# First group's output projection by Strassen pairs of 288 columns, with up weights formed beside the query pairs

## The chip, the cores and the metric

One core of a Trainium2 chip runs the kernel in one launch. The metric is the device time in microseconds (us), as the median of three runs. Of the core's engines the text names PE (TensorE, which multiplies matrices), DVE (VectorE), ACT (ScalarE), POOL (GpSimd) and SP (SyncE, whose queue issues nearly all DMAs here). Each engine works through its own instructions in order and waits on the others by semaphores.

## The reference

One decoder layer in float32 for a prompt of 1,024 tokens and a sample group of 8 x 8 tokens, which share the weights; the width is 1,024.

```python
h = rmsnorm(x, norm_mix)
q, k, v, gu, gv, ga, gb = split_in(h @ w_in)
o = attn_prompt(q, k, v, sinks)            # or attn_sample, for the sample group
vn = layernorm(jax.nn.gelu(gv), ln_g, ln_b)
s = spatial_gating(jax.nn.gelu(gu), vn, ws, bs)
merged = jax.nn.sigmoid(ga) * (o @ w_pa) + jax.nn.sigmoid(gb) * (s @ w_pb)
x = x + merged @ w_out
f, nconv = conv_ffn(rmsnorm(x, norm_ffn), w_up, conv_w, conv_b, w_down, prev)
return x + f, nk, nv, nconv, vn
```

The change is about `x + merged @ w_out`, the output projection.

## The kernel before

All activations are kept transposed: a tile has 128 of the 1,024 channels on its partitions and tokens along its columns. The 1,088 tokens are two groups: group 0 has 576 columns (64 of the sample group, 512 of the prompt), group 1 has the other 512. A float32 operand is split into a high part, rounded by ACT (`split`, L40), and a low part, the rest, by DVE (L41). A product is three matmuls: high with high, low with high, high with low.

The stages follow one another on PE: values and gMLP values, then queries, keys, gMLP inputs and gates (L297), attention with the branch products between its pieces, the merges, the first group's output projection, the second group's, the up stage (L297), the down stage (L1734) and the final norm. L237 is the matmul line of `mm3`, which the merges and both output projections share.

The stages on L297 take the weights in pairs of 128 x 1,024 tiles and multiply by Strassen's scheme (Winograd's form). A pair has 7 products in place of 8; each product is 4 blocks (`kk`) of 3 matmuls over half of a group's columns: 288 for group 0, 256 for group 1. For that a pair's weights are added to four sums (`ws`, L176) and split to seven halves of 128 x 512, and the activations to four sums (`combine`, L259 to L262) and split to seven operands per `kk`. `Chain.product` collects the products in PSUM banks, with the names "adadaca": a bank that goes on accumulating must have been copied out by ACT (`keep`, L278) first.

`Weights` (`W`) keeps the weights in order: four raw tiles (`wraw`) are loaded ahead, and `W.get` forms the next splits (`wh`, `wl`) ahead of their use in four slots.

The merge of tile c of group 1 is 48 matmuls of 256 columns; DVE then multiplies by the gate (L1094) and adds the other branch (L1096), and `operand(1)` splits the result. At the same time a merged tile of group 0 comes back from DRAM in its two parts (`m` and `b`), is added (L1397) and is split whole by `operand(0)`. So the first group's projection finds eight pairs `mh`, `ml` of 576 columns. It goes over eight output tiles, 24 matmuls of 320 and 24 of 256 columns for each, and `x1_tile` adds the tile of x, stores it and adds its square to the norm's sum (L1413, L1423).

Beside the merges and the first projection, in `pair_load` and `pair_unit`, the weights of the first NPRE = 2 pairs of the up stage are added and split (`hl`), and stored in DRAM (`upd`), from where the up stage takes them as they are.

The order on each engine isn't written out: a scheduler in the framework places the instructions from the code's order, so that matmuls of several products can be mixed.

Of the kernel before, what the change touches and what calls it, by code (L numbers as in the profile page):

```python
# [6 lines left out]
F32 = mybir.dt.float32  # L7
F32R = mybir.dt.float32r
# [7 lines left out]
P = 128  # L16
D = 1024
KD = 8
# [16 lines left out]
def layer(tc, a):  # L35
# [11 lines left out]
    with ExitStack() as top:  # L47
# [219 lines left out]
        class Chain:  # L267
# [19 lines left out]
            def product(self, j, w):  # L287
# [11 lines left out]
                kept = self.kept  # L299
# [55 lines left out]
        with ExitStack() as ph1:  # L355
# [523 lines left out]

            mo, sso = [ExitStack(), ExitStack()], ExitStack()  # L880
# [89 lines left out]
            late["qk"] = poola("qk", 1, qko)  # L970

            def behind(at, j):

                if done:
                    done.pop(0)()
# [9 lines left out]
            for at, (pair, gs, whole) in enumerate(seq):  # L985
                if at == 6:
                    qko.close()
# [38 lines left out]
            pst = ph1.enter_context(tc.tile_pool(name="pst", bufs=1, space=PSUM, reuse_waits="tile"))  # L1026
            pmm = ph1.enter_context(tc.tile_pool(name="pmm", bufs=2, space=PSUM, reuse_waits="tile"))
            psm = ph1.enter_context(tc.tile_pool(name="psm", bufs=1, space=PSUM, reuse_waits="tile"))
# [50 lines left out]
            def merge(g, c, to, early=False):  # L1079
# [3 lines left out]
                def part(e, k0):  # L1083
                    def go():
                        if e == k0 == 0:
# [4 lines left out]
                            st["w"], st["ps"] = W.get(), acc2()  # L1090
# [249 lines left out]
            hmo = [ExitStack(), ExitStack()]  # L1340
            hmp = [hmo[g].enter_context(tc.tile_pool(name=f"hm{g}", bufs=1, reuse_waits="tile")) for g in (1, 0)][::-1]

            def operand(g):
                def go(c, t):
                    hl = tuple(hmp[g].tile([P, groups[g]["n"]], F32R, name=f"m{x}{c}") for x in "hl")
                    split(*hl, t)
                    ms[g].append(hl)
                return go

            pwo, pair = ExitStack(), {}  # L1350
            pwp = pwo.enter_context(tc.tile_pool(name="pw", bufs=1, reuse_waits="tile"))

            def pair_load(f):
                def go():
                    store()
                    for e, name in enumerate("ab"):
                        pair[name] = pwp.tile([P, KD, P], F32, name=f"r{name}")
                        nc.sync.dma_start(pair[name], wt(UP0 + f + NFF * e))
                return go

            def pair_unit(f, j):

                def go():
                    store()
                    ta, tb = pair["a"], pair["b"]
                    a11, a12, a21, a22 = ta[:, 0:4], ta[:, 4:8], tb[:, 0:4], tb[:, 4:8]
                    src = {0: a11, 5: a12, 6: a22}.get(j)
                    if src is None:
                        x, y = ((a21, a22), (pair.get("s1"), a11), (pair.get("s2"), a12), (a11, a21))[j - 1]
                        src = pair[f"s{j}"] = pwp.tile([P, 4, P], F32, name="s", bufs=2)  # L1370
                        V.tensor_add(src, x, y)
                    t = pwp.tile([P, 2, 4, P], F32R, name="hl", bufs=2)
                    split(t[:, 0], t[:, 1], src)
                    pair["store"] = upd[f][j], t.bitcast(F32)
                return go

            def store():
                if "store" in pair:
                    nc.sync.dma_start(*pair.pop("store"))

            held = {}

            def hold(c):
                if c < KD:
                    held[c] = [pwp.tile([P, 576], F32, name=x, bufs=3) for x in "mb"]
                    for x, src in zip(held[c], (msd[c], mbd[0][c])):
                        nc.sync.dma_start(x, src)
# [586 lines left out]
```

## Time and profile before

| what | us |
|---|---|
| median of three runs | 1519.96 |
| lowest, highest | 1518.12, 1522.0 |
| span of the profiled execution | 1514.1 |
| its own time, beside the span | not measured apart; the span is 5.9 below the median |
| PE busy in the span | 1494.2 |
| merges of group 1 from the second on | about 680 to 714 |
| first group's output projection | 714.2 to 765.0 |
| second group's output projection | 765.0 to 811.5 |
| up stage | 811.5 to 1271 |

The span is the time from the first to the last instruction of one execution; the measured time also holds what lies around it. A row of the timeline gives an instruction's start, its duration, its engine, its line, its kind, what it writes and reads by the names of the program, its shape, and in brackets how long the engine was idle before it and what ended that. Instructions of one engine overlap in their durations, so that their cost in a chain is the distance from one start to the next.

### The profile page before, as it was taken

The numbers are of one execution on the slowest core, as the hardware profiler recorded it, in microseconds if no ns is written. First come the engines' busy times: TensorE is split into PE (matmuls) and PEld (weight loads), VectorE is DVE, ScalarE is ACT, GpSimd is POOL, SyncE is SP. The second block draws the span as 40 slices with busy tenths as digits, with TensorE's granted clock in tenths as the row PEclk, the third lists the DMA queues.
The fourth block names the chain that finished last, engine by engine and source line by source line (L and its number), as shares of the span: only waits on it lengthen the run. The fifth ranks groups of instructions, "written<-read, shape, count | busy, mean of one in ns | idle before, by whom it ended". The sixth has DMA issues, their size and how long they took to land.

```text
span 1514.1 us, 31415 instructions
## 1 busy us (share of the span) xinstructions
PE 1494.2 (99%) x12194; PEld 1481.5 (98%) x12194; DVE 1160.7 (77%) x1917; ACT 821.6 (54%) x1745; POOL 269.5 (18%) x427
## 2 busy tenths in 40 slices
PE   9999999999999999999999999999999999999997
PEld 9999999999998999999999999999999999999997
DVE  6896778756545895989668888898899888785685
ACT  7565764454543774864444555555555556353562
POOL 0000012200020222330132221332232122000003
PEclk9999999999999999999999999999999999999999
DMA  8452557747659857749988323332233226973453
GB/s 291 158 186 110 178 181 254 232 134 271 232 182 312 270 164 230 233 169 306 330 282 283 129 107 124 110 126 108 94 138 109 91 74 229 368 244 97 124 180 133
DMA packets 137508, 286.70 MB, mean 189 GB/s; under 512 B 15248, under 2 KB 44368, under 8 KB 137360
## 3 DMA queue, kind: packets, MB, share of 16 engines
q1 hardware_dynamic: 133040, 280.62, 55.1%
q10 hardware_dynamic: 4320, 4.08, 0.8%
q8 instruction: 96, 1.57, 0.4%
q14 instruction: 52, 0.43, 0.1%
HBM read 195.76 MB, written 90.85 MB: 189 GB/s over the span
## 4 chain that ended last, share of the span: by engine, by line
PE 85%; DVE 4%; ACT 4%; issue 3%; DMA 3%; POOL 1%; SPq 0%; POOLq 0%; ACTq 0%; DVEq 0%
PE st L297 49%; PE mm L237 14%; PE dn L1734 10%; PE st L528 6%; PE sc L1227 1%; DMA wraw<-wt 1%; DVE wl L41 1%; ACT s L1250 1%; PE pt L1260 1%; POOL x L1799 1%; PE mx L836 1%; PE po L1288 1%; DMA sg1d<-z 1%; ACT wh L40 1%; DVE nm L1243 0%
## 5 line engine op out<-in xcount | busy, mean ns | idle before, releaser
L297 PE MATMUL st<-th,wh 128*128 128x256 f32 (+1 forms) x2128 | 610.3, 287 | 2.1 <-ACT k L278 1.5
L297 PE MATMUL st<-tl,wh 128*128 128x256 f32 (+1 forms) x2128 | 608.4, 286 | 0.0
L297 PE MATMUL st<-th,wl 128*128 128x256 f32 (+1 forms) x2128 | 608.0, 286 | 0.0
L297 PEld LDWEIGHTS st<-th,wh 128*128 128x128 f32 x2128 | 399.9, 188 | 3.6 <-ACT k L278 2.5
L297 PEld LDWEIGHTS st<-th,wl 128*128 128x128 f32 x2128 | 400.2, 188 | 0.0
L297 PEld LDWEIGHTS st<-tl,wh 128*128 128x128 f32 x2128 | 399.7, 188 | 0.0
L41 DVE TENSOR_TENSOR wl<-wraw,wh 128x512 fp32r<-128x512 f32 (+2 forms) x204 | 158.2, 789 | 35.2 <-ACT wh L40 32.0
L40 ACT CAST wh<-wraw 128x512 fp32r<-128x512 f32 (+2 forms) x204 | 139.5, 694 | 82.3 <-PE st L297 33.5
L1734 PE MATMUL dn<-th,wh 128*128 128x288 f32 (+1 forms) x616 | 176.7, 287 | 0.0
L1734 PE MATMUL dn<-tl,wh 128*128 128x288 f32 (+1 forms) x616 | 176.2, 286 | 0.0
L1734 PE MATMUL dn<-th,wl 128*128 128x288 f32 (+1 forms) x616 | 175.1, 284 | 0.0
L40 ACT CAST wh<-ws 128x512 fp32r<-128x512 f32 x160 | 98.3, 622 | 105.2 <-PE st L297 67.9
L41 DVE TENSOR_TENSOR wl<-ws,wh 128x512 fp32r<-128x512 f32 x160 | 110.6, 704 | 48.0 <-ACT wh L40 46.1
L1734 PEld LDWEIGHTS dn<-th,wl 128*128 128x128 f32 x616 | 115.9, 188 | 0.0
L1734 PEld LDWEIGHTS dn<-tl,wh 128*128 128x128 f32 x616 | 115.7, 188 | 0.0
L1734 PEld LDWEIGHTS dn<-th,wh 128*128 128x128 f32 x616 | 115.6, 188 | 0.0
L285 POOL TENSOR_TENSOR z<-kn,k 128x256 f32<-128x256 f32 (+1 forms) x32 | 30.1, 943 | 305.0 <-ACT kn L280 287.7
L40 ACT CAST th<-traw 128x544 fp32r<-128x544 f32 (+1 forms) x85 | 53.9, 642 | 48.7 <-PE dn L1734 34.4
L41 DVE TENSOR_TENSOR tl<-traw,th 128x544 fp32r<-128x544 f32 (+1 forms) x85 | 61.5, 730 | 20.8 <-ACT th L40 20.7
L237 PE MATMUL mm<-s,wh 128*128 128x256 f32 (+1 forms) x384 | 76.4, 294 | 0.0
L528 PE MATMUL st<-w2h,th 128*128 128x256 f32 x308 | 74.1, 282 | 0.2 <-ACT w2h L40 0.2
L237 PE MATMUL mm<-ol,wh 128*128 128x256 f32 (+1 forms) x256 | 73.5, 288 | 0.4 <-DVE ol L41 0.4
(294 smaller groups left out, 3159.3 us busy)
## 6 DMA issues: line engine op xcount, KB each, us to landing
wraw<-wt SPq DMA_DIRECT2D x133, 512.0 KB
traw<-td SPq DMA_DIRECT2D x77, 272.0 KB
td<-za SPq DMA_DIRECT2D x22, 544.0 KB
wraw<-wt SPq DMA_DIRECT2D x35, 256.0 KB
upd<-hl SPq DMA_DIRECT2D x14, 512.0 KB
td<-t SPq DMA_DIRECT2D x11, 544.0 KB
qd<-q SPq DMA_DIRECT2D x8, 576.0 KB
q<-qd SPq DMA_DIRECT2D x8, 576.0 KB
```

Of the source, the lines that this page charges most:

```text
L40: S.copy(hi, src)
L41: V.tensor_sub(lo, src, hi.bitcast(F32))
L237: PE.matmul(ps[:, lo:lo + c1 - c0], u[:, k, :], v[:, c0:c1], start=(clear and k == 0 and i == 0), stop=(k == nk - 1 and i == 2), skip_grou ...
L285: op(to, pick(x, to, lo, hi), pick(y, to, lo, hi))
L297: PE.matmul(ps, u[:, kk, :], v, start=first and kk + i == 0, stop=kk == 3 and i == 2, skip_group_check=True)
L528: PE.matmul(ps, u, v[:, k, :], start=k + i == 0, stop=k == KD - 1 and i == 2)
L836: PE.matmul(ps[:, P * i:P * i + P], vn[:, i], late["wst"][:, c, :], start=True, stop=True)
L1227: PE.matmul(ps[:, h, o0:256], q, kst[kv][:, e, k0:cur + P], start=e == 0, stop=e == 1)
L1250: S.activation(s[:, h], s[:, h], AF.Exp, bias=nm[:, h:h + 1], accum_out=dn[:, h:h + 1])
L1260: PE.transpose(pt[:, h * P:h * P + P], s[:, h, 0:P], ident)
L1288: PE.matmul(half(po, e), v[:, b - 1 + e], half(x, e), start=e == 0 and x is ph, stop=False, skip_group_check=True)
L1734: PE.matmul(place(m, e), u[:, m, :], v[:, lo:hi], start=new and i + k == 0 and (e == 0 or m % 2 == 0), stop=i == NU - 1 and k == 2, skip_g ...
```

## The change

The first group's projection is done by the Strassen scheme too. Class `Out` is a `Chain` with its own way of collecting: ACT copies four of the banks (`keep`), POOL adds these copies into the two tiles of x of the pair, and DVE adds the other three straight from PSUM. There are 4 pairs (output tiles p and p + 4) of 7 products of 12 matmuls of 288 columns. W holds four pairs and then eight whole tiles in place of sixteen whole tiles.

The operands `tmh`, `tml` (seven of 288 columns for each `kk`) are formed in the merges of group 1: `entire` adds the two parts of a tile as before, `form_sums` makes the four sums of two tiles, `form_split` splits 288 and 576 columns at once and 1,152 a little later. The tiles come in the order 0, 4, 1, 5, 2, 6, 3, 7, so that each second merge has what one `kk` needs. The last merge asks W for four splits ahead, the first pair's halves.

The sums and splits of the first two up pairs' weights move to the query pairs (`up_units`, positions 1 to 4 of that stage, one unit beside every second product), with smaller loads (`px`, `py`).

Three places show the new order. First DVE at the end of the merges and the start of the first projection, before (L1094 and L1096 are the merge's multiply and add; L1371 and `hl` belong to the up weights):

```order
L1094 TENSOR_TENSOR stg<-stg,mm 128x512
L41 TENSOR_TENSOR wl<-wraw,wh 128x1024
L1096 TENSOR_TENSOR stg<-stg 128x512
L1371 TENSOR_TENSOR s<-s,ra 128x512
L41 TENSOR_TENSOR wl<-wraw,wh 128x1024
L41 TENSOR_TENSOR ml_9808<-stg,mh_9807 128x512
L41 TENSOR_TENSOR hl<-s,hl 128x512
L1371 TENSOR_TENSOR s<-ra,rb 128x512
L1094 TENSOR_TENSOR stg<-stg,mm 128x512
L41 TENSOR_TENSOR wl<-wraw,wh 128x1024
L1096 TENSOR_TENSOR stg<-stg 128x512
```

And the same place now (L1142 and L1144 are the multiply and the add of the last merge, `t` the sums of `form_sums`, `tml` the low operands of `kk` 3):

```order
L259 TENSOR_TENSOR t_9946<-m 128x288
L260 TENSOR_TENSOR t_9946<-m 128x288
L41 TENSOR_TENSOR tml_9964<-m,tmh_9963 128x288
L41 TENSOR_TENSOR wl<-ws,wh 128x512
L261 SCALAR_TENSOR_TENSOR t_9946<-t_9946,m 128x288
L41 TENSOR_TENSOR tml_9964<-m,tmh_9963 128x576
L262 SCALAR_TENSOR_TENSOR t_9946<-t_9946,m 128x288
L1142 TENSOR_TENSOR stg<-stg,mm 128x512
L176 TENSOR_TENSOR ws<-wraw 128x512
L1144 TENSOR_TENSOR stg<-stg 128x512
L41 TENSOR_TENSOR tml_9964<-t_9946,tmh_9963 128x1152
L41 TENSOR_TENSOR ml_9998<-stg,mh_9997 128x512
```

The last of the first projection's operands now stands behind the last merge's multiply and add, where before the group's operands were done ahead of them.

On PE, the first matmuls of the projection, before:

```order
L237 MATMUL mm_9898<-mh0_9320,wh_9817 128x320
L237 MATMUL mm_9898<-ml0_9321,wh_9817 128x320
L237 MATMUL mm_9898<-mh0_9320,wl_9818 128x320
L237 MATMUL mm_9898<-mh1_9382,wh_9817 128x320
L237 MATMUL mm_9898<-ml1_9383,wh_9817 128x320
```

And now, from the 19th of its matmuls on (the bank `st_10010` belongs to the pair's first product, `st_10032` to its second, `st_10109` to its sixth):

```order
L297 MATMUL st_10032<-tmh2_9804,wl_9915 128x288
L297 MATMUL st_10109<-tmh0_9496,wh_10026 128x288
L297 MATMUL st_10109<-tml0_9497,wh_10026 128x288
L297 MATMUL st_10010<-tml3_9964,wh_9914 128x288
L297 MATMUL st_10010<-tmh3_9963,wl_9915 128x288
L297 MATMUL st_10032<-tmh3_9963,wh_9914 128x288
L297 MATMUL st_10032<-tml3_9964,wh_9914 128x288
L297 MATMUL st_10032<-tmh3_9963,wl_9915 128x288
```

The matmuls that need `kk` 3 (`tmh3`, `tml3`) are put behind some that don't.

On SP, at the start of the query pairs, before:

```order
L147 DMA wraw<-wt 128x1024 x4
L860 DMA qd_114<-q 256x1x512
L860 DMA qd_115<-q 256x1x512
L147 DMA wraw<-wt 128x1024 x2
L860 DMA qd_106<-q 128x1152
```

And now:

```order
L895 DMA px<-wt 128x512
L895 DMA py<-wt 128x512
L899 DMA upd_1_183<-phl 128x1024
L895 DMA py<-wt 128x512
L899 DMA upd_6_188<-phl 128x1024
L867 DMA qd_114<-q 256x1x512
L867 DMA qd_115<-q 256x1x512
L899 DMA upd_2_184<-phl 128x1024
L869 DMA qsd<-z_1736 128x64
L147 DMA wraw<-wt 128x1024 x2
```

The loads and stores of the up weights stand between the loads of the weights that are needed next.

The diff, cut to its core:

```diff
-            for at in (PA0, PA0, WO0, WO0):
+            for at in (PA0, PA0):
                 for c in range(8):
                     W.add(wt(at + c), KD)
+            for c in range(4):
+                W.add_pair(wt(WO0 + c), wt(WO0 + c + 4))
+            for c in range(8):
+                W.add(wt(WO0 + c), KD)
...
+            def up_units(pool):
+
+                q, hold = {}, []
+
+                def load(name, f, x):
+                    src = wt(UP0 + f + NFF * (x[1] == "2"))
+                    k = 4 * (x[2] == "2")
+                    q[name] = pool.tile([P, 4, P], F32, name=name)
+                    nc.sync.dma_start(q[name], src[:, k:k + 4])
+
+                def store():
+                    if hold:
+                        nc.sync.dma_start(*hold.pop())
+
+                def step(f, j, src, add, then):
+                    def go():
+                        store()
+                        if add:
+                            V.tensor_add(q["px"], q["px"], q["py"])
+                        t = pool.tile([P, 2, 4, P], F32R, name="phl")
+                        split(t[:, 0], t[:, 1], q[src])
+                        hold.append((upd[f][j], t.bitcast(F32)))
+                        for x in then:
+                            load(*x)
+                    return go
+
+                out = [lambda: [load("px", 0, "a21"), load("py", 0, "a22")]]
+                for f in range(NPRE):
+                    more = [("px", f + 1, "a21"), ("py", f + 1, "a22")] if f + 1 < NPRE else []
+                    out += [step(f, 1, "px", True, ()), step(f, 6, "py", False, [("py", f, "a11")]),
+                            step(f, 2, "px", True, ()), step(f, 0, "py", False, [("py", f, "a12")]),
+                            step(f, 3, "px", True, [("px", f, "a21")]), step(f, 5, "py", False, [("py", f, "a11")]),
+                            step(f, 4, "px", True, more)]
+                return out + [store]
+
...
+                if ahead and at > 0 and j % 2 == 0:
+                    ahead.pop(0)()
...
-                            st["w"], st["ps"] = W.get(), acc2()
+                            st["w"], st["ps"] = W.get(4 if g and c > 6 else 1, 2 if g and c > 5 else 3), acc2()
...
+            tw, held, raw = {}, {}, {}
+            half_of = lambda t: t.rearrange("p (h c) -> p h c", h=2)
+
+            def hold(i):
+                if i < KD:
+                    c = i // 2 + 4 * (i % 2)
+                    held[i] = [hbp.tile([P, 576], F32, name=x, bufs=n) for x, n in (("m", 4), ("b", 3))]
+                    for x, src in zip(held[i], (msd[c], mbd[0][c])):
                         nc.sync.dma_start(x, src)
 
+            def entire(i):
+                t, u = held[i]
+                V.tensor_add(t, t, u)
+
+            def form_sums(kk):
+                xs = [held.pop(2 * kk + e)[0] for e in range(2)]
+                t4 = hbp.tile([P, 4, 288], F32, name="t4", bufs=2)
+                combine(t4, *(x[:, h * 288:h * 288 + 288] for x in xs for h in range(2)))
+                raw[kk] = *xs, t4
+
+            def form_split(kk, late):
+                x0, x1, t4 = raw[kk]
+                if not late:
+                    tw[kk] = tuple(tm0.tile([P, 7, 288], F32R, name=f"tm{y}{kk}") for y in "hl")
+                th, tl = tw[kk]
+                if late:
+                    split(th[:, 1:5], tl[:, 1:5], t4)
+                else:
+                    split(th[:, 0], tl[:, 0], x0[:, 0:288])
+                    split(th[:, 5:7], tl[:, 5:7], half_of(x1))
+
+            for i in range(3):
+                hold(i)
+            own1.append(operand)
             for c in range(KD):
+                kk, odd = c // 2, c % 2
+                for at, go in enumerate(merge(1, c, operand) if c else [none, none, *first[2:]]):
                     if at == 1:
+                        entire(c)
+                        if odd:
+                            form_sums(kk)
+                        else:
+                            hold(c + 3)
                     go()
+                    if odd and at == 1:
+                        form_split(kk, False)
+                        hold(c + 3)
+                    elif odd and at == 2:
+                        form_split(kk, True)
+            tx[0] = tw
...
+            class Out(Chain):
+
+                def product(self, j, w):
+                    ps, (xc, xd), n2 = self.multiply(j, w), self.places, self.n2
+                    c0, c1, d0, d1 = (x[:, n2 * h:n2 * h + n2] for x in (xc, xd) for h in range(2))
+                    kept = self.kept
+                    if j in (0, 1, 2):
+                        name, to, op = (("1", c0, G.tensor_add), ("5", d1, G.tensor_sub), ("u", c1, G.tensor_add))[j]
+                        self.keep(name, ps)
+                        op(to, to, kept[name])
+                    elif j == 4:
+                        self.keep("n", ps)
+                        G.tensor_sub(d1, d1, kept["n"])
+                    else:
+                        to, op = {3: (c1, V.tensor_add), 5: (c0, V.tensor_add), 6: (d0, V.tensor_sub)}[j]
+                        op(to, to, ps)
+
             nacc = nacc0 = rsg[0]
+            xs = [x_of(groups[0], c) for c in (0, 4)]
+            for p in range(4):
+                xc, xd = xs
+                chain = Out(0, tx, psw, xsp, (xc, xd))
+                for j in range(7):
+                    chain.product(j, W.get(3, 1))
+                    if j == 1 and p < 3:
+                        xs = [x_of(groups[0], c) for c in (p + 1, p + 5)]
+                    if j == 5:
+                        x1_out(0, p, xc)
+                x1_out(0, p + 4, xd)
+            ahead_x = [x_of(groups[1], 0)]
+            xso.close()
...
```

More of the change, by code (lines that the diff above doesn't have):

```diff
@@ L1377, in store @@
[L1377 to L1386, printed above, removed]
-                        nc.sync.dma_start(x, src)
-            hold(0)
-            hold(1)
-            ahead = [x for f in range(NPRE) for x in (pair_load(f), *(pair_unit(f, j) for j in range(7)))]
```

103 lines of the change are left out of this document (35 added, 68 removed).

## The prediction

> **What bounds the kernel now.** The page comes first: TensorE (PE) is busy for nearly the whole span, and the chain that ended last runs through it. PE's waits come second: all of them together are about 13 us, the longest 1.4.
>
> ```profile
> span 1514.1 us, 31415 instructions
> PE 1494.2 (99%) x12194; PEld 1481.5 (98%) x12194; DVE 1160.7 (77%) x1917; ACT 821.6 (54%) x1745; POOL 269.5 (18%) x427
> PE 85%; DVE 4%; ACT 4%; issue 3%; DMA 3%; POOL 1%; SPq 0%; POOLq 0%; ACTq 0%; DVEq 0%
> ```
>
> ```profile
> PE pt L1260 <- DVE s L1253: 3.5, 9, 0.9
> PE st L297 <- ACT k L278: 1.5, 2, 1.3
> ```
>
> So a matmul less counts in full, if its operands are ready. Whether they are is asked of the stages that the change touches, by busy time (columns: window, its length, then each engine's busy time and instructions, clock, DMA share, GB/s):
>
> ```profile
> 133.00:195.00 62.00, 62.00 (x505) 62.00 (x505) 44.24 (x68) 42.33 (x84) 5.17 (x6) 1.00 0.42 149
> 679.00:719.70 40.70, 40.70 (x351) 40.70 (x352) 39.03 (x56) 19.95 (x27) 0.00 (x0) 1.00 0.86 288
> 719.70:770.80 51.10, 51.10 (x396) 51.10 (x394) 27.87 (x31) 19.45 (x28) 12.66 (x9) 1.00 0.93 332
> ```
>
> The third and fourth numbers after the length are VectorE (DVE) and ScalarE (ACT). The query pairs (133 to 195) leave DVE 29% idle, the first group's projection 45%. The second group's merges just ahead of it leave DVE nothing: 39.0 of 40.7 us. That row decides the forecast, since the change gives the merges more DVE work.
>
> **Matmuls removed.** Two of the last merge's matmuls (seven starts apart), the projection's first and the next stage's first are these:
>
> ```profile
> 713.31 0.28 PE L237 MATMUL mm<-ol,wh 128*128 128x256 f32 x1
> 714.10 0.28 PE L237 MATMUL mm<-oh,wl 128*128 128x256 f32 x1
> 714.21 0.30 PE L237 MATMUL mm<-mh,wh 128*128 128x320 f32 x1
> 764.98 0.28 PE L237 MATMUL mm<-mh,wh 128*128 128x256 f32 x1
> ```
>
> The stage takes 50.77 us for 384 matmuls. The change does 4 pairs x 7 products x 12 = 336 matmuls of 288 columns. The up stage has such matmuls back to back; these two are 153 starts apart:
>
> ```profile
> 819.09 0.29 PE L297 MATMUL st<-th,wh 128*128 128x288 f32 x1
> 839.36 0.30 PE L297 MATMUL st<-th,wh 128*128 128x288 f32 x1
> ```
>
> 20.27 / 153 = 0.1325 us each, so 336 take 44.5 us: 6.3 less. (The merge's 256 stand 0.79 / 7 = 0.113 apart; at that rate per column a 288 would take 0.127 and the 312 that follow the stall below 1.7 us less. I keep the row of the same form, with 1.7 as the lower bound.)
>
> **DVE in the merges.** DVE's operations overlap, so start to start is what counts:
>
> ```profile
> 680.30 0.69 DVE L1094 TENSOR_TENSOR stg<-stg,mm 128x512 f32<-128x512 f32 x1 [0.94 <-PE mm L237]
> 680.90 0.75 DVE L1397 TENSOR_TENSOR m<-m,b 128x576 f32<-128x576 f32 x1
> 681.57 0.69 DVE L1096 TENSOR_TENSOR stg<-stg 128x512 f32<-128x512 f32 x1
> 687.25 1.22 DVE L41 TENSOR_TENSOR wl<-wraw,wh 128x1024 fp32r<-128x1024 f32 x1
> 688.39 0.75 DVE L41 TENSOR_TENSOR ml<-m,mh 128x576 fp32r<-128x576 f32 x1
> 710.58 0.69 DVE L1094 TENSOR_TENSOR stg<-stg,mm 128x512 f32<-128x512 f32 x1
> 716.80 0.68 DVE L1094 TENSOR_TENSOR stg<-stg,mm 128x512 f32<-128x512 f32 x1
> ```
>
> A 512 costs 0.60 us, a 576 0.67, a 1024 1.14. From 680.30, where DVE last waited for PE, to 710.58 there are 23, 16 and 5 of them: 13.8 + 10.7 + 5.7 = 30.2 us, against 30.28. DVE has no gap there, and the last merge is multiplied at 716.80 though its matmuls ended at 714.2. The new shapes have rows in the up stage's own preparation:
>
> ```profile
> 781.34 0.45 DVE L260 TENSOR_TENSOR t<-x,x 128x288 f32<-128x288 f32 x1
> 781.71 0.45 DVE L41 TENSOR_TENSOR tl<-x,th 128x288 fp32r<-128x288 f32 x1
> 784.92 1.35 DVE L41 TENSOR_TENSOR tl<-t,th 128x1152 fp32r<-128x1152 f32 x1
> 786.19 0.81 DVE L1484 SCALAR_TENSOR_TENSOR x<-x,c_gains,sc 128x576 f32<-128x576 f32 x1
> ```
>
> A 288 costs 0.37 us, an 1152 1.27. Out go eight first-group splits of 576 and the up weights' sums and splits. In come, for each of four kk, four sums of 288 and splits of 288, 576 and 1152, and in the last merges the first pair's weight halves. By the changed order DVE must do, from the same start up to the last operand split (`tml`, 1152, kk 3): 8 multiplies and 8 adds of the second group (9.6), 7 of its splits (4.2), 8 adds of 576 (5.4), 16 sums (5.9), 4 x (0.37 + 0.67 + 1.27) = 9.2, four weight splits of 1024 (4.6), four weight sums and four splits of 512 (4.8). That is 43.7 us: the split starts at 722.7 and ends at 680.3 + 43.7 = 724.0 to 724.1.
>
> PE reaches the projection at 714.21 as before. It can do 24 of its 336 matmuls without that split (the first product, ten of the second, two of a later one), 3.2 us, and is then out of work: to 717.0 it runs, then the first product's last two wait for `tml`'s 288 (to about 719), then the second product's last wait for the cast and the split of 1152. So PE stands for 724.06 - 717.4 = 6.7 us. ACT was busy for 19.95 us there; eight casts of 576 become four of 288, 576 and 1152, 3,456 columns more:
>
> ```profile
> L40 ACT CAST mh<-m 128x576 fp32r<-128x576 f32 x8 | 5.4, 676 | 6.6 <-DVE m L1397 6.5
> ```
>
> At 676 ns for 576 that is 4 us: some 24 of 43.7, so DVE sets the end. Behind the split stand in DVE's queue the second group's last split and the weight halves of product 4 on; PE needs the half for product 4 at about 727, DVE has it at 725.3. The rest of the first pair needs ACT's copy of the first bank, queued behind three casts: 0.3 to 0.4 us more.
>
> The stage then ends at 724.06 + 312 x 0.1325 + 0.35 = 765.75, against 764.98: the gain is gone and 0.8 with it. Bounds: -1.7 by the merges' rate, and up to +1.5 if operands or weight halves of the last merges land late.
>
> **The clock after the stall.** Nothing in the middle of this profile keeps PE waiting longer than 1.4 us. At both of its ends PE was idle, and the rows show the consequence:
>
> ```profile
> L597 PE MATMUL st<-c_ones 128*128 128x128 f32 x16 | 3.8, 431 | 1.2 <-DVE c_ones L76 1.2
> L1784 PE MATMUL fs<-dg,c_ones 128*128 128x128 f32 x8 | 1.1, 284 | 1.0 <-DVE dg L1776 1.0
> ```
>
> ```profile
> 5.18 0.88 PE L528 MATMUL st<-w2h,th 128*128 128x256 f32 x3 [0.21 <-ACT w2h L40]
> 5.90 0.28 PE L528 MATMUL st<-w2l,th 128*128 128x256 f32 x1
> ```
>
> ```profile
> 1506.00:1507.00 1.00, 0.99 (x8) 0.95 (x8) 0.33 (x2) 0.00 (x0) 0.00 (x0) 1.00 1.08 388
> 1507.00:1508.00 1.00, 0.14 (x2) 0.00 (x0) 1.00 (x4) 0.37 (x1) 0.30 (x1) 0.82 0.95 341
> 1508.00:1509.00 1.00, 0.00 (x0) 0.00 (x0) 1.00 (x3) 0.00 (x0) 1.00 (x2) 0.50 0.48 173
> ```
>
> At the end the granted clock falls to 0.50 at about 1507.64 (a mean of 0.82 in that microsecond), half a microsecond after the last matmul and some 5 after dense work ended, with 20 small matmuls between. At the start the same 128x128 form takes 431 ns instead of 284, some twice as long start to start (16 in 3.78 us against 8 in 1.13), and full speed shows at 5.9, 4.4 us after the first matmul at 1.18 (the clock column reads 1.00 there; the durations tell). A stall of 6.7 us with four matmuls in it probably does this too, and PE then comes back at half speed. 4.4 us at half speed lose 2.2. Bounds: 0, if the four matmuls keep the clock up, and 3.4 us, if it takes half as long again. I take 2.2, from the start of this kernel.
>
> The Trainium skill, "TensorE: Matmul & The Clock Gate", section "What's actually happening", says that the clock halves after an idle window of about 3.4 us and comes back after a busy one as long. By it the loss would be 1.7 us, and the sum half a microsecond less; the rows above agree with the halving, and give the longer return.
>
> **DVE and POOL in the projection.** Now POOL adds four times 288 columns a pair and 576 for the norm. In the trace such a POOL add stretched a DVE one:
>
> ```profile
> 787.00 1.52 POOL L1423 TENSOR_TENSOR nacc<-nacc,stg 128x512 f32<-128x512 f32 x1 [6.24 <-ACT stg L1422]
> 787.29 1.55 DVE L260 TENSOR_TENSOR t<-x,x 128x288 f32<-128x288 f32 x1
> ```
>
> ```profile
> L1423 POOL TENSOR_TENSOR rs<-rs,stg x7: 1492/1567/2143, 729.9 to 767.2; 128x576 f32<-128x576 f32 x7
> ```
>
> ```profile
> L285 POOL TENSOR_TENSOR z<-kn,k 128x256 f32<-128x256 f32 (+1 forms) x32 | 30.1, 943 | 305.0 <-ACT kn L280 287.7
> ```
>
> The 288 took 1.1 us longer than its 0.45; of the two groups below, the first shows the shortest, median and longest, the second the mean (943). DVE's work in a pair: 7 weight splits and 4 sums of 512 (6.6) and three adds of 288 (1.1), 7.7 of the 11.1 us that PE takes; ACT's 7 casts and 4 copies are less. Slack of 3.4 a pair hides it: 0 (the other end is a rival below).
>
> **Up weights beside the query pairs.** 14 splits and 8 sums of 512 columns on DVE, 22 x 0.60 = 13.2 us over 133 to 216, take DVE from 71% to 87%; 14 casts ACT from 68% to about 79%; 14 stores of 512 KB and 12 loads of 256 KB (10.5 MB in 83 us) bring 126 GB/s to the 149, under the 332 that the projection's row shows. SP's queue has each store behind its split and ahead of weight loads, whose four raw tiles give some 20 us of room. I put 0.3 us here; 0 to 3 are the bounds. The merges and the projection lose the same DMAs (their share was 0.86 and 0.93), which PE didn't wait for: 0.
>
> **Sum.** -6.3 + 6.7 + 0.35 + 2.2 + 0.3 = +3.2 us: a span of 1517.3. The profiled span stands 5.9 below the median of the runs; with the same distance the median becomes 1523.2.
>
> **The rivals.**
> - The gain shows: the operands are ready in time, -6.3 + 0.3: 1514. PE's 99% speaks for it; the unbroken DVE rows from 680.30 on speak against it, since more work can't end sooner. 0.04.
> - The stall without the clock: +1.0 to 1.4, 1521. For it: the four matmuls in the stall, and the end of the kernel, where 20 kept the clock for some 5 us. 0.20.
> - Slower, by DVE's whole durations: if each operation waited for the one before to be through (0.69, 0.75, 1.22, 0.45, 1.35), the 43.7 us become 49.7, the split ends at 730 and all is 6 us later: 1529. It decides as soon as over half of that shows. The starts 0.60 apart of operations that last 0.69 speak against it. 0.05. The Trainium skill, "VectorE: DVE Perf Modes", section "The DRAIN you can't avoid", states that the next operation doesn't start until the pipe is empty; the trace doesn't agree, by those rows.
> - Slower, by POOL in the projection: if each of its adds blocked DVE for its whole length (4 x 0.94 + 2 x 1.57), DVE would need 14.6 us a pair against 11.1, 3.5 a pair, 14 on top of the stall: 1535. It decides from 3.4 us of blocking a pair on. 0.04.
> - Slower, by the query pairs: DVE or ACT stands behind a late load of the up weights and PE runs out of weight halves, 2 to 3 us on top of the sum: 1525.7. 0.12.
>
> **Chances.** The forecast itself has 0.55. About what a measurement of this kernel can tell from no change is 0.3%, 4.6 us: 1515.4 to 1524.5. Faster is the first rival and a little of the second: 0.05. Slower are the last three (0.21) and a sixth of the forecast, where the clock takes the longer return: 0.31. The rest, 0.64, is within. Leaving out the first and most of the two dear rivals, the range is 1518.5 to 1527.5.
>
> **What would show it.** In the changed profile: a PE wait of 5 to 8 us in all near 717 to 724, for `tml` from L41; DVE without a gap from 680.3 to 724; the granted clock at 0.5 for 3 to 5 us from 724 on; then 288s every 0.1325 us, and the second group's first matmul at 767 to 769. The prediction is wrong if DVE has pauses in the merges, if PE starts the projection later than 714 (a wait that moved up into the merges), if the clock stays at 1.00, or if PE waits at `st` between 133 and 216.

## The result, and the profile after

The changed kernel takes 1532.17 us (median of six runs, 1527.29 to 1534.47) against 1519.89 for the kernel before: a ratio of 1.0078, 95% interval 1.0066 to 1.0091. It is slower by 12 us; the forecast was 3 slower, with a range that ended at 1527.5. The page after has these lines for the ones shown of before:

```profile
span 1527.8 us, 31473 instructions
PE 1496.8 (98%) x12146; PEld 1480.1 (97%) x12146; DVE 1192.5 (78%) x1977; ACT 837.3 (55%) x1785; POOL 290.7 (19%) x443
PE 63%; DVE 8%; DMA 5%; issue 3%; ACT 3%; POOL 1%; SPq 0%; POOLq 0%; ACTq 0%; DVEq 0%
```

PE has 48 matmuls less and yet is busy 2.6 us longer (half a clock counts as busy), and the chain that ended last leaves PE for DVE and DMAs more often. The waits of PE, of which before had nothing over 1.4 us in one piece:

```profile
PE st L297 <- ACT k L278: 5.4, 6, 1.6
PE st L297 <- ACT tmh L40: 2.7, 1, 2.7
PE st L297 <- ACT ku L278: 2.6, 4, 1.2
PE st L297 <- DVE tml L41: 2.1, 2, 1.5
```

(A wait of 2.0 us for `z` at 468.20 is new too, but three of before at that place, 2.1 us together, are gone with it.) Where the 13.7 us of span went is read from the starts of the stages, by PE's timeline:

```profile
680.13 0.41 PE L1308 MATMUL pt<-c_ident,s 128*128 128x128 f32 x2 [0.84 <-DVE s L1301]
723.16 0.29 PE L297 MATMUL st<-tmh,wh 128*128 128x288 f32 x1
779.20 0.28 PE L237 MATMUL st<-mh,wh 128*128 128x256 f32 x1
```

The first row is the last transposition of the attention, which before had at 672.53; then come the first matmuls of the two projections (714.21 and 764.98 before).

| stretch | before | after | difference |
|---|---|---|---|
| up to the attention's last transposition | 672.53 | 680.13 | +7.6 |
| from there to the first projection | 41.68 | 43.03 | +1.35 |
| first projection | 50.77 | 56.04 | +5.3 |
| the rest of the span | 749.1 | 748.6 | -0.5 |

These are single executions. The profiled one of before is short: 34 later executions of that kernel have spans of 1514.4 to 1522.5. So the medians, 12.3 us apart, tell the whole better, and a stretch is known to some 1 to 3 us (see the experiments).

**Beside the query pairs.** PE had not waited at all between 112 and 235. Now it does, for copies of PSUM banks by ACT. Two rows of ACT and one of PE show the first of these waits:

```profile
118.08 0.62 ACT L40 CAST phl<-px 128x512 fp32r<-128x512 f32 x1 [2.70 <-DVE px L905]
118.61 0.37 ACT L278 COPY ku<-st 128x256 f32<-128x256 f32 x1
```

```profile
119.03 0.38 PE L297 MATMUL st<-th,wh 128*128 128x256 f32 x1 [1.17 <-ACT ku L278]
```

The copy `ku` is what PE needs. It stands in ACT's queue behind the cast `phl` of the up weights, which waits for DVE's sum `px`, which waits for a load. What ACT and DVE waited for between 110 and 235, by their waits (total, times, longest):

```profile
ACT phl L40 <- DMA upd<-phl: 10.6, 5, 3.7
ACT phl L40 <- DVE wl L41: 4.9, 1, 4.9
```

```profile
DVE px L905 <- DMA py<-wt: 8.0, 5, 2.6
```

The first row names a store: `phl` has one buffer, and the next cast may not write it until the store before it has landed.

**At the start of the first projection.** DVE began the merges at 687.91 and split the last operands at 730.36:

```profile
687.91 0.69 DVE L1142 TENSOR_TENSOR stg<-stg,mm 128x512 f32<-128x512 f32 x1 [0.96 <-PE mm L237]
730.36 1.35 DVE L41 TENSOR_TENSOR tml<-t,tmh 128x1152 fp32r<-128x1152 f32 x1
```

```profile
687.91:731.77 43.86, 39.12 (x326) 38.44 (x324) 43.86 (x72) 21.88 (x32) 0.00 (x0) 0.98 0.67 208
731.77:779.20 47.43, 45.02 (x313) 44.08 (x314) 39.96 (x51) 24.12 (x47) 29.06 (x23) 0.94 0.53 174
```

Of these windows' columns the fifth (after PE and PEld) is DVE: busy for 43.86 of 43.86 us, without a gap. PE ran out of operands:

```profile
725.81 0.29 PE L297 MATMUL st<-tml,wh 128*128 128x288 f32 x1
726.69 0.40 PE L297 MATMUL st<-tml,wh 128*128 128x288 f32 x1 [0.58 <-DVE tml L41]
726.92 0.29 PE L297 MATMUL st<-tmh,wl 128*128 128x288 f32 x1
729.88 0.40 PE L297 MATMUL st<-tmh,wh 128*128 128x288 f32 x1 [2.66 <-ACT tmh L40]
731.77 0.61 PE L297 MATMUL st<-tml,wh 128*128 128x288 f32 x1 [1.49 <-DVE tml L41]
732.17 0.45 PE L297 MATMUL st<-tmh,wl 128*128 128x288 f32 x1
...
736.97 0.35 PE L297 MATMUL st<-tmh,wl 128*128 128x288 f32 x1
737.16 0.30 PE L297 MATMUL st<-tmh,wh 128*128 128x288 f32 x1
```

The steps from 725.81 to 731.77 hold 5.96 us for four matmuls: 5.4 us are lost. From there a 288 lasts 0.45 and starts come 0.24 apart, until 736.97. The granted clock, the last but two of these columns, says why:

```profile
730.00:731.00 1.00, 0.28 (x1) 0.07 (x1) 1.00 (x2) 1.00 (x3) 0.00 (x0) 0.63 0.79 189
731.00:732.00 1.00, 0.23 (x1) 0.23 (x2) 1.00 (x2) 1.00 (x3) 0.00 (x0) 0.50 0.26 99
736.00:737.00 1.00, 1.00 (x6) 1.00 (x6) 0.53 (x1) 0.99 (x3) 0.51 (x1) 0.50 1.04 426
737.00:738.00 1.00, 1.00 (x9) 1.00 (x9) 0.00 (x0) 0.45 (x1) 1.00 (x2) 0.96 0.64 258
```

It fell to 0.50 at about 730.3 and rose at about 737.1, after 6.8 us, 5.3 of them after PE had work again. The Trainium skill, "TensorE: Matmul & The Clock Gate", section "What's actually happening", gives about 3.4 us of activity until the clock returns; this trace has 5.3, but it agrees with the two steps, 0.50 and 1.00, and the whole stretch is twice 3.4 us.

**Later in the projection.** PE waits for copies again, four times and 2.4 us in all. The rows of POOL, ACT and PE around the first of them:

```profile
744.75 1.97 POOL L1472 TENSOR_TENSOR rs<-rs,stg 128x576 f32<-128x576 f32 x1 [3.61 <-ACT stg L1471]
746.69 2.46 POOL L1483 TENSOR_TENSOR x<-x,k 128x288 f32<-128x288 f32 x2
748.60 0.62 ACT L40 CAST wh<-ws 128x512 fp32r<-128x512 f32 x1 [2.22 <-DVE ws L176]
749.13 0.39 ACT L278 COPY ku<-st 128x288 f32<-128x288 f32 x1
749.57 0.40 PE L297 MATMUL st<-tmh,wh 128*128 128x288 f32 x1 [0.85 <-ACT ku L278]
```

The copy `ku` stands behind the cast `wh`, which waits for DVE's weight sum `ws`; DVE's rows beside POOL's adds are shown at no_pool.

### The profile page after: what moved, and what is told of

Read it like the earlier page. It is cut to its first block, busy times and chain, and to the rows that moved or that the text cites. A ratio compares the mean times of both kernels' runs of the same rounds, so it can differ in the third digit from the quotient of the medians.

```text
span 1527.8 us, 31473 instructions
## 1 busy us (share of the span) xinstructions
PE 1496.8 (98%) x12146; PEld 1480.1 (97%) x12146; DVE 1192.5 (78%) x1977; ACT 837.3 (55%) x1785; POOL 290.7 (19%) x443
## 4 chain that ended last, share of the span: by engine, by line
PE 63%; DVE 8%; DMA 5%; issue 3%; ACT 3%; POOL 1%; SPq 0%; POOLq 0%; ACTq 0%; DVEq 0%
PE st L297 40%; PE dn L1800 11%; PE mm L237 4%; PE st L237 3%; DVE wl L41 2%; DMA q<-qd 1%; PE sc L1275 1%; PE pt L1308 1%; ACT s L1298 1%; POOL x L1865 1%; DMA wraw<-wt 1%; PE mx L843 1%; PE po L1336 1%; DVE ws L176 1%; ACT wh L40 1%
## 5 line engine op out<-in xcount | busy, mean ns | idle before, releaser
L40 ACT CAST wh<-ws 128x512 fp32r<-128x512 f32 x176 | 108.2, 622 | 111.5 <-PE st L297 59.7
L41 DVE TENSOR_TENSOR wl<-ws,wh 128x512 fp32r<-128x512 f32 x176 | 124.2, 718 | 40.0 <-ACT wh L40 38.3
L278 ACT COPY k<-st 128x256 f32<-128x256 f32 (+1 forms) x160 | 59.0, 382 | 29.9 <-PE st L297 29.2
```

Of the source, the lines that this page charges most:

```text
L40: S.copy(hi, src)
L41: V.tensor_sub(lo, src, hi.bitcast(F32))
L278: S.copy(t, src)
```

## The experiments

Each run is compared with the kernel before in the same job. The two last columns are PE's stretches from the first query product to the attention's last transposition, and the first projection.

| run | median | before | ratio, 95% interval | to the attention's end | projection |
|---|---|---|---|---|---|
| before | 1519.89 | | 1 | 560.4 | 50.8 |
| changed | 1532.17 | 1519.89 | 1.0078 (1.0066 to 1.0091) | 568.2 | 56.0 |
| two_bufs | 1530.74 | 1521.06 | 1.0063 (1.0048 to 1.0078) | 564.9 | 57.3 |
| up_only | 1529.91 | 1521.06 | 1.0051 (1.0034 to 1.0069) | 570.7 | old form |
| out_dve | 1533.90 | 1521.06 | 1.0080 (1.0065 to 1.0096) | 570.0 | 55.8 |
| add_early | 1533.78 | 1521.06 | 1.0081 (1.0064 to 1.0098) | 574.6 | 50.1 |
| q_dep | 1529.19 | 1520.22 | 1.0057 (1.0035 to 1.0078) | 564.4 | 56.2 |
| no_pool | 1527.75 | 1520.22 | 1.0048 (1.0032 to 1.0064) | 569.6 | 52.4 |
| warm | 1533.44 | 1520.22 | 1.0080 (1.0060 to 1.0101) | 568.8 | 55.6 |
| dep_warm | 1526.73 | 1520.22 | 1.0048 (1.0032 to 1.0064) | 564.6 | 55.7 |
| no_sums | 1524.11 | 1520.78 | 1.0028 (1.0018 to 1.0039) | 569.0 | 50.9 |
| free | 1520.11 | 1520.78 | 0.9997 (0.9984 to 1.0010) | 571.0 | 45.0 |
| free_q | 1515.64 | 1520.00 | 0.9976 (0.9964 to 0.9988) | 565.8 | 45.1 |

The intervals reach 1.6 to 3.3 us to either side, so the stretches of the profiles say more about single steps. But each is of one execution: changed, out_dve, no_pool, warm, no_sums and free are the same kernel up to the attention's end, and have 568.2 to 571.0 there (569.4 in the mean, 9.0 more than before); q_dep, dep_warm and free_q have 564.4 to 565.8 (564.9). In the projection, changed, two_bufs and q_dep are the same and have 56.0 to 57.3. Smaller differences than these spreads tell nothing.

**up_only: the move of the up weights alone, in the kernel before.**

```diff
+            ahead = up_units(poola("pw", 1, qko))
...
-            ahead = [x for f in range(NPRE) for x in (pair_load(f), *(pair_unit(f, j) for j in range(7)))]
-                    if at == 2 and c % 2:
-                        ahead.pop(0)()
```

> The kernel before, with only the move of the up weights' sums and splits to the query pairs; the first projection is the old one. If the move alone makes the loss: about 7 us slower than before, 1527, with the same PE waits for ACT's copies between 112 and 235. Rival (the loss there comes from the changed tiles and order of the whole, not from the move): within 1.5 us of before, 1519 to 1521.

It is 8.9 us slower, and 10.3 us are lost before the attention's end, with waits for the same copies as in the changed kernel. The one at 208.22 lasts 1.99 us (1.60 there, at 207.01), and the clock then stood at half for 3.4 us (a mean of 0.87 over 210 to 220). The two projections together take 97.0 us as before (97.1): freeing DVE there bought nothing, since PE hadn't waited. So this part, which I had put at 0.3, costs 8.9 us alone, and the 10.3 lie within the spread of the changed kernel's own executions.

**two_bufs: two buffers for what is stored, and the stage ring for what is loaded.**

```diff
-                    q[name] = pool.tile([P, 4, P], F32, name=name)
+                    q[name] = stage(512).rearrange("p (k c) -> p k c", c=P)
-                        t = pool.tile([P, 2, 4, P], F32R, name="phl")
+                        t = pool.tile([P, 2, 4, P], F32R, name="phl", bufs=2)
```

> The changed kernel, but the up weights' units beside the query pairs have two buffers for what they store (phl) and take px and py from the ring of four stage tiles, so that a cast needn't wait for the store before it, nor a sum for a load into the same tile. Theory 1 (one buffer each: ACT's queue stands for 10.6 us behind stores and DVE's for 8 us behind loads, and the copies of PSUM banks stand behind them): the 7.1 us that PE lost between 112 and 235 shrink to under 2, median about 1526 against 1532. Theory 2 (the query stage is simply too full with the added sums, splits and 10.5 MB): at least 5 us of the loss stay, 1530 to 1533.

PE's waits between 112 and 235 became one:

```profile
PE st L297 <- ACT ku L278: 2.0, 1, 2.0
```

That is the first load, at 119.68; half a clock followed it (0.84 over 120 to 130). The later waits are gone: they came from the single buffers. But 4.5 us of loss stay up to the attention's end, where under 2 were expected, most of them behind that first wait and its half clock; the median is 9.7 above before, against 12.3, and didn't fall to 1526.

**q_dep: as two_bufs, and the first loads wait for a late result.**

```diff
+                    if "dep" in late:
+                        V.tensor_copy(q[name][:, 0, 0:1], late["dep"][:, 0:1])
                     nc.sync.dma_start(q[name], src[:, k:k + 4])
...
+                    late.pop("dep", None)
...
+                if at == 1:
+                    late["dep"] = zs[1][1]
```

(The copy makes the loads depend on that result, so that the scheduler can't place them earlier.)

> As two_bufs (two buffers for phl, px and py from the stage ring), and the first loads wait for the last result of the first query pair (a copy of one column into their tiles), so that the first unit comes some 15 us later, when the weight loads ahead of it on SP's queue have landed. Two_bufs still lost 4.3 us at 117 to 123: 1.95 of waiting for the first load, and then half a clock for 3.4 us. Theory 1b (the late first load is that rest): PE has no wait over 0.5 us between 112 and 235, the clock stays at 1.00 there, the stage loses under 1 us to before; median 1525 against before's 1520. Theory 2 (the stage is too full): 3 us or more of loss stay, 1528 or more.

```profile
PE st L297 <- ACT k L278: 0.6, 2, 0.4
```

PE's waits there fall from 4.6 to 0.6 us, the clock stays at 1.00, and the stretch to the attention's end from +7.7 to +4.0. The expectation of under 1 us of loss fails: by the count of `st<-th,wh` started between 112 and 300 (500 before, 482 changed, 493 here, three matmuls of 0.124 each) about 2.6 us of 6.7 stay, and the median, 1529.19, is in the range of theory 2. PE does the same matmuls in the same order as in before, so the rest can be placed one by one: 2.1 us up to 205, of which 0.6 are waits; 0.8 more up to 277, for a longer wait for `k` (2.3 us against 1.3); and 0.9 in the attention, mostly a wait of 0.7 for a load of `q`. So about half of the loss (4.5 of 9.0 us by the means above) was buffers and a late load; where the other half lies is known, its cause is open.

**add_early: the two parts of a merged tile are added in the attention.**

```diff
-                            if g:
-                                V.tensor_add(st["t"], st["t"], st["u"])
+                            V.tensor_add(st["t"], st["t"], st["u"])
...
-                t, u = held[i]
-                V.tensor_add(t, t, u)
```

> The changed kernel, but the two parts of a merged tile of the first group are added when the first part is made, in the second group's attention, so that 8 adds of 576 and 8 loads leave the second group's merges. By the order DVE then needs 35.8 us, not 43.7, from its first multiply there to the last operand split. Theory 4 (the stall and the half clock come from DVE's lag in the merges): PE waits under 1 us at the start of the projection, the granted clock stays at 1.00, and the median falls by 6 to 7.6, to about 1525. Rival (the 5.4 us of adds come back in the attention, where DVE is busy for 81%): it falls by less than 3, to 1529 to 1532, with more PE waits between 470 and 680. A second rival (the clock falls for another reason than the stall) would show 0.50 at the same place.

Theory 4's stall and clock came true, and so did the rival's waits; the median didn't fall (12.7 us above before, against 12.3), which is under both forecasts' gains. The projection takes 50.1 us, 5.9 less, without a stall at its start and at full clock. The attention pays for it:

```profile
PE pt L1306 <- DVE s L1299: 5.6, 11, 1.9
```

(3.5 in nine waits in the changed kernel), the clock falls twice (at 470.4 and 685.5), and the stretch up to its end is 6.4 us longer.

**out_dve: the projection's adds of copied banks on DVE.**

```diff
-(("1", c0, G.tensor_add), ("5", d1, G.tensor_sub), ("u", c1, G.tensor_add))[j]
+(("1", c0, V.tensor_add), ("5", d1, V.tensor_sub), ("u", c1, V.tensor_add))[j]
-                        G.tensor_sub(d1, d1, kept["n"])
+                        V.tensor_sub(d1, d1, kept["n"])
```

> The changed kernel, with the four adds of copied banks in each pair of the projection on DVE, straight after the copy, and not on POOL. Theory 3 (POOL's adds stretch DVE's, so that weight sums come late, ACT's casts wait for them and the bank copies stand behind): PE's four waits for copies from 749 on (2.4 us, 3.1 with the restarts) go, median about 1529. Rival (DVE is full by its own count, and 1.5 us more a pair make it worse): 1532 to 1534.

The stage stays at 55.8 us: a wait for `ku` of 1.89 us replaces four shorter ones. Neither forecast can be told from this, since DVE got the adds that POOL lost: 16 of 288 columns at 0.37 are 5.9 us, while what its 512s last beyond 0.69 fell from 8.4 to 2.1 us in all. The median, 1533.90, is the rival's.

**no_pool: POOL's work in the projection left out** (the adds of copied banks and the first group's sum of squares).

```diff
-                        op(to, to, kept[name])
-                        G.tensor_sub(d1, d1, kept["n"])
-                    G.tensor_add(nacc, nacc, sq)
+                    if g:
+                        G.tensor_add(nacc, nacc, sq)
```

> The changed kernel without POOL's work in the first projection: the four adds of copied banks a pair and the first group's sum of squares are left out, the copies by ACT stay. Theory 3 (contention with POOL makes DVE late for the weight sums): DVE's 512s there all start 0.60 apart again, PE's waits for copies from 745 on are gone, and the stage is 3 us shorter (53 us against 56.0). Rival (DVE is late by its own count, which out_dve's lack of a gain would fit): less than 1 us shorter.

52.4 us, 3.7 less, and no wait for a copy is left. DVE's rows show what POOL did; first the changed kernel, beside the POOL rows shown above, then this one:

```profile
745.52 1.76 DVE L41 TENSOR_TENSOR wl<-wraw,wh 128x512 fp32r<-128x512 f32 x1
747.20 1.30 DVE L176 TENSOR_TENSOR ws<-ws,wraw 128x512 f32<-128x512 f32 x1
748.42 1.28 DVE L41 TENSOR_TENSOR wl<-ws,wh 128x512 fp32r<-128x512 f32 x1
```

```profile
751.75 0.69 DVE L176 TENSOR_TENSOR ws<-wraw 128x512 f32<-128x512 f32 x1
752.49 0.69 DVE L41 TENSOR_TENSOR wl<-ws,wh 128x512 fp32r<-128x512 f32 x1
```

From 731.77 to the end of the stage 13 of DVE's 36 operations of 512 columns last over 0.8 us in the changed kernel, here none. The buffers of the copies, which POOL reads, aren't the reason for the waits: ACT's copies (L278) wait there for PE alone.

**warm: 32 more matmuls in the stall, whose results aren't used.**

```diff
+                    if p == 0 and j == 1:
+                        warm = acc2()
+                        for i in range(32):
+                            PE.matmul(warm[:, 0:288], w[0][:, 0, :], tw[i % 3][0][:, 0], start=i == 0, stop=i == 31,
+                                      skip_group_check=True)
```

> The changed kernel with 32 more matmuls of 288 columns into a spare bank at the start of the first projection, on operands that are ready, so that PE works on through its stall; their results are not used. Theory 5 (the half clock follows from the stall): the granted clock stays at 1.00 and the stage is 2 to 2.5 us shorter, 53.6 us against 56.0, though it has 32 matmuls more. Rival (the clock falls with the load or the copies): 0.50 shows as before and the stage is as long or longer.

The first half is right: the clock stays at 1.00. The second is wrong: the stage takes 55.6 us. Columns as above, 723 to 743:

```profile
723.00:733.00 10.00, 9.09 (x66) 8.44 (x64) 10.00 (x18) 6.29 (x11) 0.00 (x0) 1.00 0.33 106
733.00:743.00 10.00, 10.00 (x77) 10.00 (x77) 9.22 (x15) 4.39 (x10) 6.40 (x4) 1.00 0.31 118
```

PE at full clock comes earlier to the next pairs' weights and waits there for copies that stand behind DVE's late sums: 3.6 us of waits for `k`, `ku` and `kn` against 2.4. Of the stall's waits 0.9 us are left, so the added matmuls (4.2 us) fit into it. The clock's loss was real and hidden; that DVE sets the end instead is asked of no_sums.

**dep_warm: q_dep and warm together.**

```diff
+ q_dep's lines and warm's lines
```

> q_dep and warm together. If both parts are what the traces say and don't depend on each other: before's median plus 12.3 - 6.5 - 2.3 = +3.5, 1523.5; the projection then still has the stall, the copies' waits and the merges' DVE. If it comes to before or under it, the stall is worth less than I count.

1526.73, +6.5 against the +3.5 expected. By the stretches it is q_dep's (564.6, against 564.4) and warm's (55.7): the two parts add, but they were counted too high. q_dep's is 3 to 4.5 us, not 6.5, and warm's about 0.4, which the spread can't tell from nothing, not 2.3.

**no_sums: plain halves for the projection's 16 weight sums.**

```diff
+                if name not in self.sums and self.units[self.emitted][0] in self.plain:
+                    ta, tb = self.raw[self.units[self.emitted][0]]
+                    self.sums[name] = {"s1": ta[:, 0:4], "s2": ta[:, 4:8], "s3": tb[:, 0:4], "s4": tb[:, 4:8]}[name]
...
+            W.plain = range(len(W.items), len(W.items) + 4)
```

> The changed kernel without the 16 weight sums (ws) of the first projection's four pairs: plain halves stand in their place, so that DVE has 9.6 us less in the merges' end and the projection, and PE, ACT's casts and POOL the same as before. Theory 6 (DVE's queue sets the end of merges and projection together, so that warm's full clock gained nothing): the stall at the projection's start is 1.8 to 2.4 us shorter, the waits for copies nearly go, and the stage takes 50 to 52 us against 56.0. Rival (stall and clock on PE set the end): 53 to 54.

50.9 us: 5.1 less for 9.6 us of DVE work, with the work of PE, ACT's casts and POOL unchanged, though the clock fell here too (0.80 over 730 to 740). The stall's waits are 3.2 us against 4.8, a little less gained than expected, and none for a copy is left. So it was DVE that set the end.

**free: without the sums, POOL's adds, the sum of squares and the merges' adds of 576.**

```diff
+ no_sums' lines and no_pool's lines
-                V.tensor_add(t, t, u)
```

> The changed kernel without three loads on DVE: the 16 weight sums of the projection's pairs, POOL's adds and the first group's sum of squares (as in no_pool), and the eight adds of 576 in the merges (with their loads). Theory 6: PE finds its operands ready, waits under 0.5 us in the projection, keeps its clock, and the stage takes 336 x 0.1325 = 44.5 to 45.5 us: 6 less than the old projection's 50.8. Rival (something else in the new form costs, such as the bank copies or the matmuls' rate): 47 or more. The query stage keeps its loss of 8 to 10 us.

```profile
724.88 0.29 PE L300 MATMUL st<-tmh,wh 128*128 128x288 f32 x1
769.91 0.28 PE L240 MATMUL st<-mh,wh 128*128 128x256 f32 x1
```

45.03 us for 336 matmuls, and no wait of PE in the stage. The six microseconds (5.7) are there when nothing else is in the way; the whole still only equals the kernel before, because the query stage, unchanged here, takes them.

**free_q: free with q_dep's lines.**

```diff
+ free's lines and q_dep's lines
```

> free with the later up weights of q_dep: what the new form would be worth if neither loss were there. Left out are the 16 weight sums, POOL's adds, the first group's sum of squares and the eight adds of 576. If the two losses are apart and free's lack of a gain (1520.1 against 1520.8) is the query stage alone: 3.3 us less than free as between q_dep and the changed kernel, up to 5.5 less by the PE's offsets (8.9 against 5.0 us up to the attention, and its stall), so 1515 to 1517 against before's 1520.5: faster. Rival (free's time is set elsewhere, or the query stage's remaining loss grows with it): 1519 or more.

1515.64, 4.4 us faster than before, as expected. It is no kernel to use, since it leaves work out, but from 12.3 us slower to 4.4 faster the two losses are accounted for: the query stage, of whose loss about half is left here (565.8), and DVE's work around the projection. None of the versions that do all the work beats the kernel before.

## Why the prediction was wrong, point by point

The sum was +3.2 us of span; it is +13.7 in the profiles and +12.3 in the medians. The misses, by the profiles: +7.3 before the attention's end, +1.35 in the merges, +2.3 in the projection, -0.5 elsewhere.

- Matmuls removed, 44.5 us for 336: right (45.0 in free).
- DVE in the merges, 43.7 us up to the last operand split: right, 730.36 - 687.91 = 42.45 up to its start against 42.4 forecast.
- The stall, 6.7 us: 5.4. The merges' 256s started 0.118 apart in this run and 0.113 before, so that PE came 1.35 us later to the same split. What the merges lost the stall gave back. That is luck and no part of the change: no_sums and free have the changed merges at 0.114, up_only the old ones at 0.118. The 0.35 for a copy behind three casts didn't show: PE waits for no copy in this stage before 749.
- The clock, 2.2 us: 22 matmuls at 0.24 instead of 0.1325, 2.4 us of PE time. Right in mechanism and size (though 5.9 - 1.18 is 4.7, not the 4.4 that I took), but warm shows that the stage gains no more than about 0.4 without it. The step that failed is to add it to the sum, as if PE set the end of the stage. The rival that left the clock out expected 1.00, which didn't come.
- "DVE and POOL in the projection", put at 0: this failed, by 3.7 us (no_pool). I set 7.7 us of DVE against 11.1 us of PE per pair and called the rest slack, but DVE entered the stage with a debt (PE began it at 723.16, DVE the last operand split at 730.36, 7.2 us later), and POOL's adds (29 us of them) made a 512 beside them last 1.3 to 1.8 instead of 0.69. The rival on POOL named the mechanism; it put its price at 14.
- "Up weights beside the query pairs", put at 0.3 with 3 as the end of its range: this step made the prediction wrong. I added occupancy, 71% to 87% for DVE and 68% to 79% for ACT, and took the free share as room. The order of the queues decides: each unit is load, sum, cast, split, store through one buffer each, and ACT's cast of a unit stands ahead of the bank copies that PE waits for. What I called SP's room of 20 us says nothing on a wait in ACT's queue. The sign that I had named, a wait of PE at `st` between 133 and 216, was there: 1.60 us at 207.01. The rival on the query pairs had the place and half of the mechanism (ACT and DVE behind a late load, but PE out of weight halves, where it waited for banks to be copied), at 2 to 3 us and 0.12; up_only has 10.3. Stores through one buffer were in neither.
- The gain in time, as a rival: excluded rightly, by the DVE rows. The one with DVE's whole durations too: starts are 0.60 apart here as before. The Trainium skill, "VectorE: DVE Perf Modes", section "The DRAIN you can't avoid", which stands beside this rival, goes on that an operation that is not held starts earlier; the prediction left that out, and the starts 0.60 apart fit it.
- The median: I put 5.9 us between the span and the median. In the runs that list both, an execution's time is mostly 1.7 to 2.0 us over its span; the rest of the 5.9 was that the profiled execution of before was a short one. For the changed kernel the distance is 4.4.

## What to carry to other kernels

An engine's idle share is no room for work that waits. Before moving a load, sum, cast and store beside another stage, write down in what order the receiving engines will issue them, how many buffers each step has, and which instruction that the bound engine waits for stands behind them. And when one engine enters a stage with a debt, compare the work of both engines over the stretch in which the debt is paid, not the stage's own sums: a loss on the other engine may be hidden, and its repair brings nothing.

## What the runs showed of the hardware that I hadn't expected

- Stalls of less than 2 us can halve PE's clock: 1.95 us at 119.68 in two_bufs and 1.79 at 283.93 in out_dve were followed by 3.4 us at 0.50 (means of 0.84 over 120 to 130 and 0.83 over 280 to 290), while 2.01 us at 468.20 in the changed kernel and 2.67 at 471.62 in free were not. The Trainium skill, "TensorE: Matmul & The Clock Gate", section "What's actually happening", speaks of a free-running window of 3.4 us; the length of the halved stretch fits (3.4 us, or twice that at the first projection), and that like stalls end differently fits a window that doesn't start with the stall. No run here settles how much idle time it takes.
- The same stream of 256-column matmuls has two speeds, both at a granted clock of 1.00. In the merges before and after:

```profile
689.73 0.28 PE L237 MATMUL mm<-oh,wh 128*128 128x256 f32 x1
690.53 0.28 PE L237 MATMUL mm<-ol,wh 128*128 128x256 f32 x1
```

```profile
699.72 0.28 PE L237 MATMUL mm<-oh,wl 128*128 128x256 f32 x1
700.54 0.28 PE L237 MATMUL mm<-oh,wh 128*128 128x256 f32 x1
```

Seven starts take 0.80 us and 0.82 us here, 113.4 and 117.8 ns over the whole stage. One speed can hold for tens of microseconds; in before it changed within one stream without a wait, at about 115. In the down stage two_bufs, up_only, out_dve, add_early and q_dep had the slower one, the others the faster; it makes 3 us of span, as much as some of the effects here, and is why the stretches of the profiles are compared stage by stage. The 1.35 us in the merges are the same thing. What chooses the speed stays open.
